# A four-mixer decoder layer with a mixture of experts: expert-weight loads held back behind the first gathered rows, and the last tile's normed rows made by VectorE

## The chip, the cores and the metric

One core of one Trainium2 chip. The metric is device time in microseconds of one execution of the whole program; three runs of the kernel before gave 1354.38 us at the median (1353.21 to 1356.09). All times below count from the start of the profiled span.

## The reference, cut to what matters

The layer has one token mixer (depth is 1, so only the stick-breaking attention runs) and then a hierarchical mixture of experts over 1024 tokens of width 1024:

```
h = rms_norm(x, norm_g[0]) * (1 + sc1) + sh1
x = x + g1 * sb_mixer(h)                       # attention, 16 heads of 64, then w_out
h = rms_norm(x, norm_g[1]) * (1 + sc2) + sh2   # "h2" below: 8 tiles of 128 tokens
grp    = argmax(h @ w_grp + b_grp)             # 1 of 4 groups
top_i  = top_k(softmax(exp_logits of grp), 2)  # 2 of the group's 8 experts
y_e    = (silu(h_e @ w_gate[e]) * (h_e @ w_up[e])) @ w_down[e]     # 32 experts, d_ff 512
x = x + g2 * sum(gate * y_e)
return rms_norm(x, final_g)
```

All is float32. sh, sc and g are six rows of 1024 made from c by one matrix product. Each expert gets the tokens that chose it, 64 on average.

## The kernel before, in words

The kernel writes every engine's instructions in the order of the Python text (`tc.manual_schedule()`), and each engine and each DMA queue works through its own in that order. A tile is taken from one pool of 49 blocks of 512 KB (`free_b`, first in first out); what first writes a block waits until all earlier users of that block are done.

Attention comes first. Then `o_stream` (lines 898 to 943) walks over the 8 tiles of 128 tokens: `o_unit(t)` multiplies by w_out and makes the residual x1 (stored to DRAM by GpSimd's queue) and u = x1 times the scale row; `h2_unit(t)` makes the normed, modulated rows h2 = u * rstd + sh2 and stores them to `h2_d` in DRAM, again on GpSimd's queue; `r_logits`, `r_pick`, `r_gate`, `r_pos`, `r_slot` and `r_table` route the tile's tokens. For the last tile (t = 7) these stand alone in lines 1045 to 1060, and nothing else is left for TensorE. Then `tables` (line 1066) gives the index lists, and `gather` (line 1078) has GpSimd's queue fetch an expert's 128 rows from `h2_d` into one of three tiles `xg`. The first three gathers stand in line 1213, behind the store of the last h2 tile.

The experts' weights are cut into 192 units of two loads of 512 KB each (list `MU`, lines 858 to 863): four "gu" units (gate and up) per expert and two "dn" units (down). The order is gu of expert 0, gu of expert 1, dn of expert 0, gu of expert 2, dn of expert 1 and so on, so units 0 to 7 are gu, 8 and 9 are dn of expert 0, 10 to 13 gu of expert 2. `m_load(n)` issues the two loads on SyncE's queue. `m_fill(reserve, upto)` loads further units while blocks are free; in `o_stream` (line 942) and in line 1047 it stops at LFIRST = 13 units, in the main loop (lines 1225, 1244) it goes on to the end, to a reserve of four.

`m_split(n)` splits a unit's two tiles into a high and a low part (ScalarE casts, line 121, VectorE subtracts, line 124), since each product is three matmuls. `xt_unit(e)` transposes the gathered rows and splits them too (lines 1107, 1109, 1110). The main loop (lines 1221 to 1250) takes unit n: 12 matmuls on TensorE (`gu_mm`, lines 1123 to 1127, or `dn_mm`, line 1164), then `m_split(n + 2)`, then `m_fill`. At n = 8, ahead of expert 0's down product, line 1241 loads the gate row `g2r` = `mod_row(3)` on the same SyncE queue. At n = 9 `y_unit(0)` (line 1176, VectorE) multiplies expert 0's result by it and scatters it to DRAM; `m_split(10)` and `m_split(11)` stand ahead of it on VectorE, `m_split(12)` behind it.

Of the kernel before, what the change touches and what calls it, by code (L numbers as in the profile page):

```python
# [16 lines left out]
AF = mybir.ActivationFunctionType  # L17
ALU = mybir.AluOpType
# [6 lines left out]
NT = T // P  # L25
# [6 lines left out]
EPS = 1e-6  # L32
NBLK = 46
RO = 6
LFIRST = 13
LOG = ()
RM = 4
SLEAD = 2
# [23 lines left out]
def decoder_layer(ctx, tc, x, c, ada_w, ada_b, norm_g, final_g, w_in, w_out, w_grp, b_grp,  # L62
                  w_exp, b_exp, w_gate, w_up, w_down, out, dbg=None):
    nc = tc.nc
# [18 lines left out]
    def take(slots, shape, dt, nm):  # L83
        cnt[0] += 1
        if not slots:
            raise RuntimeError(f"no slot for {nm}: " + str(collections.Counter(v[3] for v in held.values() if v[1] is slots)))
        pool, tag = slots.popleft()
        t = pool.tile(list(shape), dt, tag=tag, name=f"{nm}{cnt[0]}")
        held[id(t)] = (t, slots, (pool, tag), nm)
        return t  # L90

    def free(*tiles):
        for t in tiles:
            _, slots, tag, _ = held.pop(id(t))
            slots.append(tag)

    def blk(shape=(P, 1024), dt=F32, nm="b"):
        return take(free_b, shape, dt, nm)

    def pm(shape=(P, 512), nm="pm"):  # L100
        return take(free_m, shape, F32, nm)
# [536 lines left out]
    OR, XR, OT, ROW = {}, {}, {}, {}  # L638
# [42 lines left out]
    def l_transpose(t, src, q):  # L681
        if q == 0:
            ST[t] = blk((P, ND, P), nm="sT")
        pt = pm((P, 4, P))
        for j in range(4):
            nc.tensor.transpose(pt[:, j, :], src[:, (4 * q + j) * P:(4 * q + j + 1) * P], ident)  # L686
        nc.scalar.copy(ST[t][:, 4 * q:4 * q + 4, :], pt)
        free(pt)
# [57 lines left out]
    def h2_unit(t):  # L746
        u, rstd = H2[t]
        h2 = blk(nm="h2")
        if t < NT - 1:
            nc.vector.scalar_tensor_tensor(h2, u, rstd, ROW["sh2"], op0=ALU.mult, op1=ALU.add)  # L750
        else:
            nc.scalar.activation(h2, u, AF.Copy, scale=rstd)
            nc.gpsimd.tensor_tensor(h2, h2, ROW["sh2"], op=ALU.add)
        nc.gpsimd.dma_start(h2_d[t * P:(t + 1) * P, :], h2)
        if dbg == "h2":
            nc.sync.dma_start(out[0, t * P:(t + 1) * P, :], h2)
        free(h2)
# [106 lines left out]
    RAW = {}  # L864
    SPL = {}

    def m_load(n):
        if n >= len(MU):
            return
        kind, e, q = MU[n]  # L870
        rs = []
        for j in range(2):
            if kind == "gu":
                r = blk((P, 2, 512), nm="wr")
                nc.sync.dma_start(r, (w_gate, w_up)[j][0, e, q * 256:(q + 1) * 256, :].rearrange(
                    "(p k) f -> p k f", p=P))
            else:
                r = blk(nm="wr")
                nc.sync.dma_start(r, w_down[0, e, (q + j) * P:(q + j + 1) * P, :])
            rs.append(r)  # L880
        RAW[n] = rs

    nload = [0]

    def m_fill(reserve, upto=LFIRST):
        while len(free_b) - 2 >= reserve and nload[0] < min(upto, len(MU)):
            m_load(nload[0])
            nload[0] += 1

    def m_split(n):  # L890
        if n >= len(MU):
            return
        rs = RAW.pop(n)
        SPL[n] = [split(r, lo_eng="g" if (n % 6 in LOG and j == 1) else "v") for j, r in enumerate(rs)]
# [3 lines left out]
    def o_stream():  # L898
        for t in range(NT):
            for k, _ in enumerate(o_unit(t)):  # L900
# [6 lines left out]
                if t == 0:  # L907
                    if k in (2, 4):
                        l_transpose("sh2", ROW["sh2"], k // 2 - 1)
                    elif k == 6:  # L910
                        pl = l_mm("sh2")
                        nc.vector.tensor_tensor(cb, pl[:, 0:40], br, op=ALU.add)
                        free(pl)
                else:
                    if k == 2:
                        h2_unit(t - 1)
                    elif k == 4:
                        l_transpose(t - 1, H2[t - 1][0], 1)
                    elif k == 7:
                        r_logits(t - 1)  # L920
                    elif k == 8:
                        r_pick(t - 1)
                        r_gate(t - 1)
                    if t == NT - 1 and k == 14:
                        r_pos(t - 1)
                        r_slot(t - 1)
# [24 lines left out]
    for n_, _ in enumerate(first):  # L951
        k, r = divmod(n_ - AD0, AD1)
# [91 lines left out]
        return  # L1044
    run_all(ost)
    t = NT - 1
    m_fill(0)
    l_transpose(t, H2[t][0], 1)
    h2_unit(t)
    free(*ROW.values())  # L1050
    r_logits(t)
# [26 lines left out]
    def gather(xg, idx):  # L1078
        nc.gpsimd.indirect_dma_start(out=xg[:, :], out_offset=None, in_=h2_d[:, :],  # L1079
                                     in_offset=bass.IndirectOffsetOnAxis(ap=idx, axis=0),  # L1080
                                     bounds_check=T - 1, oob_is_err=False)
# [14 lines left out]
    def x_chunk(xg, c):  # L1096

        k0 = c // 2 * 256 + c % 2
        return xg[:, k0:k0 + 255:2]

    def xt_unit(e):
        xg = xgs[e % 3]
        h, l = blk((P, ND, P), F32R, nm="xTh"), blk((P, ND, P), F32R, nm="xTl")
        for q in range(2):
            pt = pm((P, 4, P))
            for j in range(4):
                nc.tensor.transpose(pt[:, j, :], x_chunk(xg, 4 * q + j), ident)  # L1107
            sl = slice(4 * q, 4 * q + 4)
            nc.scalar.copy(h[:, sl, :], pt)  # L1109
            nc.vector.tensor_tensor(l[:, sl, :], pt, h[:, sl, :], op=ALU.subtract)  # L1110
            free(pt)
        XT[e] = (h, l)
# [104 lines left out]
    for n in range(SLEAD):  # L1217
        m_split(n)
    xt_unit(0)
    gather(xgs[0], gidx[:, 3:4])  # L1220
    for n, (kind, e, q) in enumerate(MU):
        if kind == "gu":
# [38 lines left out]
    with tc.If(nx > 0):  # L1261
        with tc.For_i(0, nx, 1) as j:
# [24 lines left out]
            for q in range(4):  # L1287
                for s, src in enumerate((w_gate, w_up)):
                    r = blk((P, 2, 512), nm="owr")
# [19 lines left out]
            for f in range(NF):  # L1309
                r = blk(nm="owr")  # L1310
# [74 lines left out]
```

## Time and profile before

| | |
|---|---|
| Median of three runs | 1354.38 us |
| The profiled execution: device time, span | 1353.67 us, 1351.9 us |
| TensorE matmul busy | 1226.3 us (91%) |
| VectorE busy | 1143.2 us (85%) |
| ScalarE, GpSimd busy | 816.3 us (60%), 307.7 us (23%) |
| Bytes moved by DMA | 306.69 MB, mean 227 GB/s |
| The expert stage | about 726 to 1304 us |

The busy share is an average over stages. The seam between attention and experts, about 704 to 728 us, is the one stretch in the middle of the program in which TensorE has little to do; the page's line of 40 slices shows it as a "6" among nines, and the granted clock there falls to 0.5 of full speed.

### The profile page before, as it was taken

How to read it: one execution, taken by the hardware profiler on the slowest of the kernel's cores; microseconds unless marked ns; L12 is line 12 of the kernel's file. 1: busy time of each engine (PE TensorE's matmuls, PEld its weight loads, DVE VectorE, ACT ScalarE, POOL GpSimd, SP SyncE). 2: the span in 40 equal slices, each digit the busy share in tenths (PEclk: the TensorE clock that was granted, in tenths of full speed). 3: DMA queues.
4: the chain of work that ended last, by engine and by line, in shares of the span. 5: the costliest groups of instructions: out<-in, count | busy, mean ns of one | idle time of the engine just before them, and what ended most of it. 6: DMA issues, size and time to landing. Idle time of an engine off the chain costs nothing.

```text
span 1351.9 us, 19350 instructions
## 1 busy us (share of the span) xinstructions
PE 1226.3 (91%) x6788; PEld 986.7 (73%) x6788; DVE 1143.2 (85%) x1485; ACT 816.3 (60%) x1177; POOL 307.7 (23%) x349
## 2 busy tenths in 40 slices
PE   3999999999999997699995999999999999999950
PEld 2886767677877775478874878888888888888840
DVE  4879989876777658967776999999999999999967
ACT  4734544555655546742225777777777777777833
POOL 2711222222222214413322232111111111111002
PEclk9898999999999999899996999999999999999985
DMA  9242434300110102467359889999999999999367
GB/s 360 82 140 67 136 99 144 122 25 28 51 44 7 42 9 105 126 231 270 125 177 366 318 322 390 386 384 396 388 381 386 377 377 387 376 383 385 139 249 293
DMA packets 123396, 306.69 MB, mean 227 GB/s; under 512 B 16976, under 2 KB 49816, under 8 KB 123296
## 3 DMA queue, kind: packets, MB, share of 16 engines
q1 hardware_dynamic: 110256, 275.99, 55.7%
q0 software_dynamic: 11776, 25.20, 5.2%
q10 hardware_dynamic: 1264, 4.23, 0.8%
q8 instruction: 54, 0.88, 0.3%
q14 instruction: 46, 0.38, 0.1%
HBM read 288.58 MB, written 33.57 MB: 238 GB/s over the span
## 4 chain that ended last, share of the span: by engine, by line
issue 37%; PE 9%; POOL 8%; DMA 2%; DVE 1%; ACT 0%; POOLq 0%; SPq 0%; DVEq 0%; ACTq 0%
POOL y_d L1086 5%; POOL xg L1079 2%; PE z L112 2%; PE z L114 2%; PE z L113 2%; PE pm L696 1%; DMA xg<-h_d,tbgi 1%; PE pm L686 1%; DMA h_d<-h 1%; DMA yb<-y_d 1%; POOL frstd L1343 0%; DMA y_d<-ys,tbsi 0%; PE pm L536 0%; PE pm L563 0%; DVE S L521 0%
## 5 line engine op out<-in xcount | busy, mean ns | idle before, releaser
L124 DVE TENSOR_TENSOR lo<-wr,hi 128x1024 fp32r<-128x1024 f32 x384 | 446.7, 1217 | 11.0 <-ACT hi L121 7.6
L121 ACT CAST hi<-wr 128x1024 fp32r<-128x1024 f32 x384 | 380.6, 1051 | 17.6 <-PE pm L1164 7.0
L521 DVE TENSOR_TENSOR_SCAN S<-S 128x128 f32<-128x128 f32 (+3 forms) x192 | 190.7, 1034 | 10.6 <-POOL S L503 8.2
L1123 PE MATMUL z<-hi,xTh 128*128 128x512 f32 x512 | 161.9, 397 | 0.2 <-ACT xTh L1109 0.2
L1125 PE MATMUL z<-lo,xTh 128*128 128x512 f32 x512 | 160.0, 393 | 1.1 <-DVE lo L124 1.0
L1127 PE MATMUL z<-hi,xTl 128*128 128x512 f32 x512 | 158.8, 391 | 0.1
L1164 PE MATMUL pm<-hi,hhl 128*128 128x512 f32 x512 | 150.2, 396 | 0.0
L537 ACT COPY aT<-pm 128x512 f32<-128x512 f32 (+2 forms) x192 | 80.8, 496 | 87.4 <-PE pm L536 86.7
L501 POOL TENSOR_SCALAR_AFFINE_SELECT S<-S 128x256 f32<-128x256 f32 x64 | 52.2, 816 | 312.7 <-ACT S L497 290.3
L1125 PEld LDWEIGHTS z<-lo,xTh 128*128 128x128 f32 x512 | 96.4, 188 | 23.5 <-DVE lo L124 2.7
L1127 PEld LDWEIGHTS z<-hi,xTl 128*128 128x128 f32 x512 | 96.3, 188 | 21.4 <-DVE xTl L1110 0.4
L112 PE MATMUL pm<-hTh,hi 128*128 128x512 f32 x256 | 108.2, 423 | 3.2 <-DVE qk L405 3.2
L1086 POOL DMA_INDIRECT y_d<-ys,tbsi x32 | 67.6, 2114 | 188.1 <-DVE ys L1176 188.1
L497 ACT ACTIVATE S<-z 128x256 f32<-128x256 f32 (+3 forms) x96 | 79.0, 823 | 50.0 <-PE z L494 17.5
L1123 PEld LDWEIGHTS z<-hi,xTh 128*128 128x128 f32 x512 | 94.1, 189 | 18.6 <-ACT xTh L1109 0.6
L1164 PEld LDWEIGHTS pm<-hi,hhl 128*128 128x128 f32 x512 | 94.1, 189 | 18.1
L1079 POOL DMA_INDIRECT xg<-h_d,tbgi x32 | 35.3, 1105 | 304.9 <-PE pm L1107 297.0
L522 DVE TENSOR_TENSOR p<-p,S 128x256 f32<-128x256 f32 (+3 forms) x96 | 96.6, 1006 | 8.8 <-DVE S L521 0.2
L536 PE MATMUL pm<-ident,p 128*128 128x128 f32 x576 | 80.2, 284 | 25.6 <-DVE p L522 18.9
L114 PE MATMUL pm<-hTh,lo 128*128 128x512 f32 x256 | 101.4, 396 | 0.2 <-POOL lo L124 0.2
L113 PE MATMUL pm<-hTl,hi 128*128 128x512 f32 x256 | 101.1, 395 | 0.0
L536 PEld LDWEIGHTS pm<-ident,p 128*128 128x128 f32 x576 | 67.5, 145 | 36.8 <-issue 22.1
(217 smaller groups left out, 2259.1 us busy)
## 6 DMA issues: line engine op xcount, KB each, us to landing
wr<-in_moe_w_gate_dram SPq DMA_DIRECT2D x128, 512.0 KB
wr<-in_moe_w_up_dram SPq DMA_DIRECT2D x128, 512.0 KB
wr<-in_moe_w_down_dram SPq DMA_DIRECT2D x128, 512.0 KB
ad<-in_ada_w_dram SPq DMA_DIRECT2D x32, 512.0 KB
ada<-in_ada_w_dram SPq DMA_DIRECT2D x16, 512.0 KB
wq<-in_sb_w_in_dram SPq DMA_DIRECT2D x16, 512.0 KB
x<-in_x_dram SPq DMA_DIRECT2D x8, 512.0 KB
wv<-in_sb_w_in_dram SPq DMA_DIRECT2D x8, 512.0 KB
```

The costliest lines, as they stand in the source:

```text
L112: nc.tensor.matmul(pt, lh, rh, start=start, stop=False)
L113: nc.tensor.matmul(pt, lh, rl, start=False, stop=False)
L114: nc.tensor.matmul(pt, ll, rh, start=False, stop=stop)
L121: nc.scalar.copy(hi, raw)
L124: (nc.vector if lo_eng == "v" else nc.gpsimd).tensor_tensor(lo, raw, hi, op=ALU.subtract)
L521: nc.vector.tensor_tensor_scan(r, r, r, s[:, h, n:n + 1], op0=ALU.mult, op1=ALU.bypass)
L536: nc.tensor.transpose(pt[:, j, :], p[:, h, j * P:(j + 1) * P], ident)
L1086: s = nc.gpsimd.indirect_dma_start(out=y2_d[:, :], out_offset=bass.IndirectOffsetOnAxis(ap=idx, axis=0), in_=ys[:, :], in_offset=None, bou ...
L1123: nc.tensor.matmul(gu[:, s, :], xh_[:, k, :], sp[s][0][:, k2, :], start=k == 0, stop=False)
L1125: nc.tensor.matmul(gu[:, s, :], xh_[:, k, :], sp[s][1][:, k2, :], start=False, stop=False)
L1127: nc.tensor.matmul(gu[:, s, :], xl_[:, k, :], sp[s][0][:, k2, :], start=False, stop=k == ND - 1)
L1164: nc.tensor.matmul(py[nh], a[:, f, :], sp[j][b][:, ns], start=f == 0 and a is hth and b == 0, stop=f == NF - 1 and a is htl)
```

## The change

Four edits. LFIRST becomes 8, so that the loads ahead of the routing stop at units 0 to 7. The call `m_fill(0)` ahead of the last tile goes. Behind `xt_unit(0)` units 8 to 12 are loaded by `m_load(n, True)`, which first has VectorE write one column of zeros into each block: the load of that block is then ordered behind that write, and the write stands on VectorE behind the split of the first gathered rows. And h2 of the last tile is made as that of the other seven, by one VectorE operation, in place of ScalarE and then GpSimd.

```diff
-LFIRST = 13
+LFIRST = 8
+LHOLD = 13
     def h2_unit(t):
         u, rstd = H2[t]
         h2 = blk(nm="h2")
-        if t < NT - 1:
-            nc.vector.scalar_tensor_tensor(h2, u, rstd, ROW["sh2"], op0=ALU.mult, op1=ALU.add)
-        else:
-            nc.scalar.activation(h2, u, AF.Copy, scale=rstd)
-            nc.gpsimd.tensor_tensor(h2, h2, ROW["sh2"], op=ALU.add)
+        nc.vector.scalar_tensor_tensor(h2, u, rstd, ROW["sh2"], op0=ALU.mult, op1=ALU.add)
         nc.gpsimd.dma_start(h2_d[t * P:(t + 1) * P, :], h2)
-    def m_load(n):
+    def m_load(n, hold=False):
...
                 r = blk((P, 2, 512), nm="wr")
+                if hold:
+                    nc.vector.memset(r[:, 0, 0:1], 0.0)
                 nc.sync.dma_start(r, (w_gate, w_up)[j][0, e, q * 256:(q + 1) * 256, :].rearrange(
...
                 r = blk(nm="wr")
+                if hold:
+                    nc.vector.memset(r[:, 0:1], 0.0)
                 nc.sync.dma_start(r, w_down[0, e, (q + j) * P:(q + j + 1) * P, :])
...
     t = NT - 1
-    m_fill(0)
     l_transpose(t, H2[t][0], 1)
...
     xt_unit(0)
+    while nload[0] < LHOLD:
+        m_load(nload[0], True)
+        nload[0] += 1
     gather(xgs[0], gidx[:, 3:4])
```

## Rows read from the trace of the kernel before

**Rows 1.** Stretches: length, busy by engine with counts, granted clock, DMA share, GB/s.
```profile
718.00:727.00 9.00, 0.51 (x3) 0.54 (x4) 3.78 (x4) 0.83 (x1) 4.08 (x3) 0.50 1.03 411
...
730.00:732.00 2.00, 2.00 (x7) 1.54 (x7) 1.96 (x2) 0.99 (x3) 0.00 (x0) 0.71 0.57 221
...
765.00:775.00 10.00, 10.00 (x50) 8.14 (x49) 9.79 (x14) 6.92 (x9) 3.59 (x2) 1.00 0.99 361
...
900.00:950.00 50.00, 50.00 (x239) 41.73 (x238) 49.03 (x52) 39.18 (x46) 8.25 (x6) 1.00 1.01 387
```

**Rows 2.** Chain that ended last, across the seam: start, duration, what.
```profile
705.61 0.55 POOL rstd L742
...
707.64 2.34 POOL h L753
...
710.27 6.98 DMA h_d<-h
```

**Rows 3.** Timeline of the seam, all engines: start, duration, instruction, [idle before <-releaser].
```profile
708.97 1.04 DVE L783 TENSOR_SCALAR inl<-iogrp,gf 128x32 f32<-128x32 f32 x1
...
714.12 0.19 DVE L1070 SCALAR_TENSOR_TENSOR tbgi<-tbl,tbw 128x32 int32<-128x32 f32 x1
...
717.16 4.62 DVE L124 TENSOR_TENSOR lo<-wr,hi 128x1024 fp32r<-128x1024 f32 x4
718.14 1.21 POOL L1079 DMA_INDIRECT xg<-h_d,tbgi  x1 [7.28 <-DMA h_d<-h]
...
726.49 1.95 PE L1107 MATMUL pm<-ident,xg 128*128 128x128 f32 x8 [9.48 <-DMA xg<-h_d,tbgi]
...
728.26 1.22 PE L1123 MATMUL z<-hi,xTh 128*128 128x512 f32 x2
```

**Rows 4.** Timeline of an earlier tile's routing, VectorE.
```profile
655.72 0.24 DVE L783 TENSOR_SCALAR inl<-iogrp,gf 128x32 f32<-128x32 f32 x1
```

**Rows 5.** DMAs by tile: an x1 store at 690 us, a gather at 742 us.
```profile
L733 POOL DMA_DIRECT2D x_d<-x x1: 559/559/559, 690.3 to 690.3; - x1
DMA to landing us min/median/max: 2.9/2.9/2.9
...
L1079 POOL DMA_INDIRECT xg<-h_d,tbgi x1: 992/992/992, 742.2 to 742.2; - x1
DMA to landing us min/median/max: 4.7/4.7/4.7
```

**Rows 6.** Timeline of SyncE's DMA queue: issues of weight loads and of g2r.
```profile
693.39 8.40 SPq L879 DMA_DIRECT2D wr<-in_moe_w_down_dram  x4
...
754.13 0.42 SPq L875 DMA_DIRECT2D wr<-in_moe_w_up_dram  x1
754.64 0.38 SPq L630 DMA_DIRECT2D g2r<-mod_d  x1
```

**Rows 7.** Timelines of VectorE and TensorE around expert 0's result.
```profile
761.55 1.41 DVE L1176 SCALAR_TENSOR_TENSOR ys<-pm,tbl,g2r 128x512 f32<-128x512 f32 x2
762.87 4.62 DVE L124 TENSOR_TENSOR lo<-wr,hi 128x1024 fp32r<-128x1024 f32 x4
...
766.56 0.63 PE L1125 MATMUL z<-lo,xTh 128*128 128x512 f32 x2
...
780.27 0.50 PE L1125 MATMUL z<-lo,xTh 128*128 128x512 f32 x1 [0.63 <-DVE lo L124]
```

**Rows 8.** Timeline of the last stage: four loads queued one behind another, the fourth's use.
```profile
1309.78 0.34 SPq L1329 DMA_DIRECT2D ya<-y_d  x1
...
1311.17 0.37 SPq L1330 DMA_DIRECT2D yb<-y_d  x1
...
1318.23 1.22 DVE L1337 TENSOR_TENSOR x<-yb,ya 128x1024 f32<-128x1024 f32 x1
```

**Rows 9.** VectorE groups by shape: busy, mean ns of one, idle before.
```profile
L750 DVE SCALAR_TENSOR_TENSOR h<-u,rstd,sh2r 128x1024 f32<-128x1024 f32 x7 | 9.0, 1280 | 0.7 <-POOL rstd L742 0.7
...
L132 DVE MEMSET ones<- 128x1 f32 x1 | 0.1, 59 | 0.7 <-PEq L1374 0.7
```

## The prediction

> **What bounds the kernel now.** I read the stretches first [rows 1]. In the expert stage (900 to 950 us) TensorE is busy for 50.00 of 50 us, VectorE for 49.03, and the DMA engines' share is 1.01: TensorE sets the pace, VectorE is 2% behind, and a delay of either is not made up. In the seam (718 to 727 us) TensorE does 0.51 us of work while DMA moves 411 GB/s. The chain of waits [rows 2] and the timeline of all engines [rows 3] say why. The last tile's rstd is ready at 706.16 (705.61 + 0.55), GpSimd has h2 ready at 709.98, its store takes 6.98 us; the first gather starts at 718.14, having waited 7.28 us for that store; TensorE transposes the gathered rows from 726.49, and the first expert matmul starts at 728.26, which I call T0. Then I read SyncE's queue [rows 6], which nobody in the seam waits for: from 693.39 to 754.13 it issues 34 loads, units 8 to 24, and right behind them, at 754.64, g2r. VectorE multiplies expert 0's result by g2r at 761.55, T0 + 33.3, with no wait shown [rows 7].
>
> **The change, part by part.**
>
> *h2 by VectorE.* ScalarE's cast and GpSimd's addition go; one VectorE operation of 1.28 us [rows 9] starts when rstd is there, 706.2 to 706.3, and ends at about 707.55, where GpSimd ended at 709.98: the store starts 2.4 us earlier. VectorE loses nothing, since its next work, the routing chain, starts behind the logits at about 708. The chain also gains: its step L783 took 1.04 us and ended just when GpSimd's addition did [rows 2, 3], against 0.24 us in an earlier tile [rows 4]. The index list, ready at 714.31 before, is ready 0.8 us earlier, at 713.5.
>
> *No loads in the seam.* The store lasted 6.98 us among weight loads; an x1 store of the same 512 KB with little beside it took 2.9 us [rows 5]. At 3 to 4 us h2 lands by 711.8, ahead of the index list: that is late next. The gather starts at about 713.9 (713.5 and 0.4 of handing over), 4.2 us earlier than 718.14. It took 8.3 us (718.14 to 726.49) with DMA full; one at 742 us took 4.7 [rows 5]. I take 4.7, which has the traffic nearest to the new one; with 8.3 as the other end it lands between 718.6 and 722.2. The matmuls start 1.8 us behind it, as before (726.49 to 728.26): T0 becomes 720.4, and 7.9 us are won there.
>
> *The gate.* The ten memsets stand on VectorE behind the two splits of units 0 and 1 and the split of the gathered rows. The first takes 4.62 us from 717.16 [rows 3], now from 716.4 to 721.0; the second is two operations of 128x512, at 0.7 us each (two of that shape take 1.41 us in rows 7), so the first memset comes at about 722.4. Memsets are short (59 ns for 128x1, rows 9), some 0.6 to 1 us in all; the lo part of unit 2, queued behind them, is wanted some 7 us behind T0, so that costs nothing. If the gather takes its other end, all this is some 3 us later. SyncE's loads start there, and bytes flow about 1 us later, 723.5 (an allowance).
>
> *What that queues.* This is the step that decides. The number of units loaded ahead of g2r in the text is set by counting blocks, not by time: the fill takes blocks down to the same reserve in every step, and behind the held loads unit 12 is the last loaded, as it was before. So again units up to 24 stand ahead of g2r: 17 units of 1.049 MB, 17.83 MB, and g2r's own 0.52 MB. Three gathers pass in the same time at some 0.26 MB each (of the page's 25.20 MB on the software queue, 8.39 MB are 16 stores of 512 KB; the rest over 64 gathers and scatters). Sum 19.1 MB. At 411 GB/s [rows 1] that is 46.5 us: 770.0. That a queue serves its loads in order the last stage shows: the fourth of the loads issued from 1309.78 on, itself issued at 1311.17, is used at 1318.23 [rows 8], 8.4 us behind the first issue, where 4 x 0.524 MB at 411 GB/s with 1 us to start would give 6.1. Some of that comes from loads behind it; I add 1.3 us. g2r is then there at 771.3.
>
> VectorE comes to that multiplication at T0 + 33.3 = 753.7 and stands still until 771.4. Queued behind it are the splits of unit 12 and all later ones; units 10 and 11 are split ahead of it, so TensorE goes on through them and stops about 759. In the trace of before VectorE's sequence from 761.55 on has hardly a gap (9.79 of 10 us in 765 to 775, rows 1), and TensorE is waiting for its lo parts at 780.27 [rows 7], so there TensorE has no slack: the sequence starts 771.4 - 761.55 = 9.85 us later than before, and the rest of the program with it. The 7.9 us won at T0 are lost inside the standstill.
>
> *The clock.* Behind an idle stretch TensorE starts at half clock: granted 0.50 (1.2 GHz) in 718 to 727, and 0.71 on average in 730 to 732 [rows 1], so the step to 2.4 GHz came at about 731, 4.7 us behind 726.49. After a standstill of 15 us the same 4.7 us cost 2.35 us of TensorE's work. It restarts when unit 12's lo parts are there, 771.4 + 1.3 + 2.4 = 775.1, where it was at 766.56: 8.5 us later, and with the clock 10.9. Most of the 1.05 us over 9.85 is covered by the waits for VectorE that TensorE had anyway (0.63 us at 780.27 and shorter ones). I charge 0.35 us.
>
> The sum: 9.85 + 0.35 = 10.2 us. The profiled execution took 1353.67 us, of it 1351.9 span; it becomes 1363.9. The median of the runs shown is 0.7 us above that execution, so the forecast is 1364.6 us.
>
> A rule of the Trainium skill bears on the rate: rows show 411 GB/s in the seam and 387 in the expert stage. DMA: Bandwidth & Descriptors, Anatomy of one DMA, puts the moving of a transfer at bytes / 436e9 plus about 2 us fixed. By it 19.1 MB would be an estimated 43.8 us, g2r would come 2.7 us earlier and the time would be 1361.9; I take the row, since no stretch read here reached that rate. The same page's Rules for kernel authors advise issuing a DMA early and waiting for it late, which speaks against holding the loads; the row of g2r's issue says what else is held with them.
>
> **The bounds.** Early end: 420 GB/s, nothing for interleaving, a free clock: 723.5 + 45.5 = 769.0, 7.45 us later than before, 1361.8; a gate 1 us earlier than I think, 1360.8. Late end: 387 GB/s (49.4 us), the late gather (3 us) cut to 2 for the part of it that could fall together, 2 us for interleaving and the whole clock (1.05): 723.5 + 2 + 49.4 + 2 = 776.9, 15.4 + 1.05 = 16.4 us later, 1370.8. Not all of these fall together.
>
> **The rivals.**
>
> 1. *g2r is no hindrance.* Were it there by T0 + 33.3 = 753.8, the whole gain at T0 would stay: 7.9 us less some 0.3 for the memsets, 1346.8. That takes at most 30.3 us of transfers behind the gate, 12.4 MB at 411 GB/s, ten units and the rest, where I count 17. For it speaks that the seam's waits are read plainly from the rows, and that before g2r lands with time to spare, within 6.9 us of its issue [rows 6, 7]; against it the count of 34 loads. Chance 8%.
>
> 2. *A part of the queue passes g2r, or the gate opens earlier.* The break-even is g2r at 761.55, and what lies between gives 1354 to 1361: for 1358 it must be there at about 765, two or three units fewer. Chance 5% for slower than 1357.1, and 3% for times within 0.2%.
>
> 3. *The hold does not hold.* If the loads started in the seam as before, the contention would stay, and only the earlier h2 would count: at most the 2.4 us of the store's earlier start, 1352.0, within 0.2%. The order on VectorE speaks against it. Chance 1%.
>
> 4. *The weights themselves run out.* Unit 8 should land some 6 us behind T0 and is wanted for its split some 17 us behind it (six units of twelve matmuls at some 0.23 us), so the ten held loads have to come one at a time, at 2.9 us each in place of 1.28, to matter: g2r then comes 16 us later still, near 1381. Chance 3%.
>
> The forecast's case has 80%. Together: slower by over 0.2% (2.7 us, about what a measurement of this kernel can tell from no change) 0.88, within 0.2% 0.04, faster 0.08. The range that holds 8 in 10 is the forecast case's own, 1360.5 to 1370.
>
> **What would show it.** Right: the first gather starts near 714 and lands in under 6 us; the first expert matmul is near 720.5; no weight load is issued between 694 and 722; VectorE then has one wait of 14 to 20 us for DMA at line 1176's counterpart for expert 0, ended by g2r at 768 to 776; TensorE idles from about 759 to 775 with the clock at 0.5, and everything behind keeps its old distances. Wrong: no such wait (rival 1), a wait of VectorE or ScalarE on a weight load (rival 4), or a first gather that still starts behind 717 (rival 3). The forecast falls if fewer than about 14 units stand ahead of g2r in SyncE's queue, or if g2r lands much earlier than its place in it says.

## The result, and the profile after

The changed kernel takes 1366.32 us at the median of four runs (1363.50 to 1368.12), the kernel before 1354.35 in the same series: a ratio of 1.0085, 95% interval 1.0064 to 1.0107. It is slower by 12 us; the forecast was 1364.6. The profiled execution took 1367.35 us, its span is 1365.5 us, 13.6 more than before.

The seam in the timeline of the changed kernel (start, duration, instruction, idle before and what ended it). In these rows PE is TensorE, DVE VectorE, POOL GpSimd and SPq SyncE's DMA queue; L and a number is a line of the kernel's text. This execution comes to the seam 0.71 us earlier than that of before (rstd starts at 704.90, where [rows 2] have 705.61), so 0.71 is to be added where a time is held against the forecast's:

```profile
704.90 0.55 POOL L743 TENSOR_TENSOR rstd<-ms,mhalf 128x1 f32<-128x1 f32 x1 [0.39 <-DVE ms L741]
705.49 1.28 DVE L750 SCALAR_TENSOR_TENSOR h<-u,rstd,sh2r 128x1024 f32<-128x1024 f32 x1 [0.67 <-POOL rstd L743]
707.07 0.58 POOL L751 DMA_DIRECT2D h_d<-h  x1 [1.61 <-DVE h L750]
707.94 0.24 DVE L780 TENSOR_SCALAR inl<-iogrp,gf 128x32 f32<-128x32 f32 x1
712.29 0.19 DVE L1071 SCALAR_TENSOR_TENSOR tbgi<-tbl,tbw 128x32 int32<-128x32 f32 x1
713.34 1.10 POOL L1080 DMA_INDIRECT xg<-h_d,tbgi  x1 [5.69 <-DVE e L811]
717.89 1.95 PE L1108 MATMUL pm<-ident,xg 128*128 128x128 f32 x8 [2.71 <-DMA xg<-h_d,tbgi]
719.66 1.22 PE L1124 MATMUL z<-hi,xTh 128*128 128x512 f32 x2
...
721.14 0.08 DVE L880 MEMSET wr<- 128x1 f32 x4
721.17 0.17 DVE L874 MEMSET wr<- 128x1 f32 x6
721.26 1.89 SPq L881 DMA_DIRECT2D wr<-in_moe_w_down_dram  x4
```

The gather now waits for VectorE, where it waited for the store [rows 3]; the profile names L811, a VectorE operation a little behind the index list of L1071. The gather lands 4.55 us behind its start, where that took 8.35. From rstd's start to the first expert matmul it is 14.76 us, and was 22.65: the seam is 7.89 us shorter. Right behind the memsets SyncE begins with the held loads. Some 40 us later its queue, VectorE's timeline, and TensorE's around the standstill show this:

```profile
760.59 0.33 SPq L875 DMA_DIRECT2D wr<-in_moe_w_up_dram  x1
761.92 0.33 SPq L631 DMA_DIRECT2D g2r<-mod_d  x1
```
```profile
751.28 2.35 DVE L125 TENSOR_TENSOR lo<-wr,hi 128x1024 fp32r<-128x1024 f32 x2
772.20 1.41 DVE L1177 SCALAR_TENSOR_TENSOR ys<-pm,tbl,g2r 128x512 f32<-128x512 f32 x2 [18.57 <-DMA g2r<-mod_d]
773.53 4.62 DVE L125 TENSOR_TENSOR lo<-wr,hi 128x1024 fp32r<-128x1024 f32 x4
```
```profile
757.99 0.71 PE L1124 MATMUL z<-hi,xTh 128*128 128x512 f32 x2
774.80 0.80 PE L1126 MATMUL z<-lo,xTh 128*128 128x512 f32 x1 [16.10 <-DVE lo L125]
775.93 0.80 PE L1126 MATMUL z<-lo,xTh 128*128 128x512 f32 x1 [0.34 <-DVE lo L125]
```

The reader is to see the order: VectorE has split unit 11 and stands still for 18.57 us for one load of 512 KB, g2r; TensorE does the two units that are split, starts unit 12 with its high part, and waits 16.10 us for the low one. The rows of stretches and clock that go with it (length, busy of TensorE, its weight loads, VectorE, ScalarE, GpSimd, granted clock, DMA share, GB/s):

```profile
740.00:750.00 10.00, 10.00 (x52) 8.49 (x50) 8.82 (x9) 7.94 (x10) 0.13 (x1) 1.00 1.03 411
...
760.00:765.00 5.00, 0.00 (x0) 0.00 (x0) 0.00 (x0) 0.00 (x0) 0.00 (x0) 0.66 1.03 413
765.00:770.00 5.00, 0.00 (x0) 0.00 (x0) 0.00 (x0) 0.00 (x0) 0.00 (x0) 0.50 1.02 407
...
774.00:776.00 2.00, 0.86 (x2) 0.36 (x2) 2.00 (x3) 1.22 (x2) 1.84 (x2) 0.50 0.99 395
776.00:778.00 2.00, 2.00 (x5) 1.61 (x6) 2.00 (x2) 1.25 (x2) 0.00 (x0) 0.50 0.67 260
778.00:780.00 2.00, 2.00 (x9) 1.60 (x8) 2.00 (x4) 1.47 (x2) 0.00 (x0) 0.83 0.41 164
```

From 760 to 770 all four compute engines are idle while DMA is full at 407 to 413 GB/s, with weights that nobody wants yet. When TensorE comes back at 774.80 it has the half clock (0.50, 1.2 GHz) up to about 778.7, some 4 us.

The last expert's result in the kernel before and in the changed one:

```profile
1304.40 1.41 DVE L1176 SCALAR_TENSOR_TENSOR ys<-pm,tbl,g2r 128x512 f32<-128x512 f32 x2 [3.22 <-PE pm L1164]
```
```profile
1315.89 1.41 DVE L1177 SCALAR_TENSOR_TENSOR ys<-pm,tbl,g2r 128x512 f32<-128x512 f32 x2 [3.17 <-PE pm L1165]
```

Where the 13.6 us of span come from, read from the same rows of both traces: 0.71 us less ahead of the seam; 11.36 more from rstd's start to expert 0's result (67.30 against 55.94 us); 0.84 more from there to the last expert's result (1315.89 - 772.20 = 543.69 us; before 1304.40 - 761.55 = 542.85); 2.1 more behind it (from the last expert's result to the end of the span). That last stretch lasted 46.8 to 49.6 us in the ten traces of this study, whatever had been changed, and rstd's start lay between 702.8 and 706.7: these two are the scatter of single executions.

### The profile page after: what moved, and what is told of

The parts are those of the page before. It is cut to its first block, busy times and chain, and to the rows that moved or that the text cites. A ratio compares the mean times of both kernels' runs of the same rounds, so it can differ in the third digit from the quotient of the medians.

```text
span 1365.5 us, 19358 instructions
## 1 busy us (share of the span) xinstructions
PE 1230.2 (90%) x6788; PEld 989.6 (72%) x6788; DVE 1145.5 (84%) x1496; ACT 815.3 (60%) x1176; POOL 300.2 (22%) x348
## 4 chain that ended last, share of the span: by engine, by line
issue 38%; PE 9%; POOL 7%; DMA 1%; DVE 1%; POOLq 0%; ACT 0%; SPq 0%; ACTq 0%; DVEq 0%
POOL y_d L1087 5%; POOL xg L1080 2%; PE z L113 2%; PE z L115 2%; PE z L114 2%; PE pm L697 1%; PE pm L687 1%; DMA yb<-y_d 1%; PE pm L564 0%; POOL frstd L1347 0%; PE pm L537 0%; DMA xg<-h_d,tbgi 0%; DMA y_d<-ys,tbsi 0%; PE tblp L843 0%; PE z L495 0%
## 5 line engine op out<-in xcount | busy, mean ns | idle before, releaser
L1087 POOL DMA_INDIRECT y_d<-ys,tbsi x32 | 64.2, 2007 | 206.9 <-DVE ys L1177 206.9
```

What stands on the lines that cost most here:

```text
L1087: s = nc.gpsimd.indirect_dma_start(out=y2_d[:, :], out_offset=bass.IndirectOffsetOnAxis(ap=idx, axis=0), in_=ys[:, :], in_offset=None, bou ...
```

## The experiments

Each kernel ran beside the kernel before on one chip; ratios are to that, with their 95% intervals.

**1. The gate row first.** The changed kernel, with g2r asked for ahead of the held loads.

```diff
     xt_unit(0)
+    g2r = mod_row(3, "g2r")
     while nload[0] < LHOLD:
...
-                if e == 0:
-                    g2r = mod_row(3, "g2r")
```

> The changed kernel with one load moved: the gate row g2r is asked for just ahead of the held loads (units 8 to 12) instead of behind unit 24. Theory (the row's place in the queue is the whole loss): the 18.6 us wait of VectorE at expert 0's result is gone, TensorE runs through from its first expert matmul at about 719.7 us, and the 7.9 us won at the seam stay: 1354.4 - 7.9 = about 1346.5 us, 20 us under the changed kernel. Rival (holding 1 MB units back starves the expert stage, and the row is only where it shows first): the wait moves to a split that waits for its weight load, with most of the 18 us still there: 1358 to 1366 us.

1348.95 us (before 1353.47), ratio 0.9974 (0.9963 to 0.9985): faster than either kernel. The queue of SyncE, VectorE's and TensorE's timeline:

```profile
699.29 0.33 SPq L631 DMA_DIRECT2D g2r<-mod_d  x1
722.20 1.85 SPq L881 DMA_DIRECT2D wr<-in_moe_w_down_dram  x4
```
```profile
720.47 1.22 PE L1124 MATMUL z<-hi,xTh 128*128 128x512 f32 x2
```
```profile
752.22 2.36 DVE L125 TENSOR_TENSOR lo<-wr,hi 128x1024 fp32r<-128x1024 f32 x2
754.50 1.40 DVE L1177 SCALAR_TENSOR_TENSOR ys<-pm,tbl,g2r 128x512 f32<-128x512 f32 x2
```
```profile
1300.10 1.41 DVE L1177 SCALAR_TENSOR_TENSOR ys<-pm,tbl,g2r 128x512 f32<-128x512 f32 x2 [3.21 <-PE pm L1165]
```

The load needs no memset, so it is issued in the quiet stretch ahead of the seam. The standstill is gone and no split of this kernel waits for its weights: the rival, that holding the loads starves the stage, falls. But 1346.5 was expected. Expert 0's result is 7.05 us earlier than before, the last expert's only 4.30: the distance between the two is 545.60 us against 542.85. No wait explains it: between the two results TensorE is idle for 2.58 us in all, and for 2.66 in the kernel before. What grew is the distance from the start of one 512-column matmul to the start of the next. It is 224 to 238 ns in nearly all cases in either trace, most often 227; but of 2107 such distances (those over 300 ns left out) 823 are 231 ns or longer here, and 460 in the kernel before. Their sum is 483.77 us against 481.00, and that is the whole difference of 2.75 between the two stages. Experiments 5 and 6 go after that.

**2. The row first, nothing held.** The same move in the kernel before.

```diff
     xt_unit(0)
+    g2r = mod_row(3, "g2r")
     gather(xgs[0], gidx[:, 3:4])
...
-                if e == 0:
-                    g2r = mod_row(3, "g2r")
```

> The kernel before with the same one load moved to the same place in the text (behind the first gathered rows' split), nothing held. Theory: the row was in time before (asked for at 754.6 us, wanted at 761.6 us), so nothing changes: 1354 us, within 0.2%. Rival (the row's early place is worth something by itself, so that the first run's gain is not the hold's): 1350 us or less.

1356.15 us, ratio 1.0014 (1.0002 to 1.0026): no gain, rather 0.1% lost. So the first experiment's gain does not come from the row's early place by itself. The seam is as before (22.71 us from rstd's start to the first expert matmul), and the small loss is again along the experts: 544.07 us from the first result to the last.

**3. Three units fewer ahead of the row.** The changed kernel, with g2r asked for at n = 5.

```diff
     for n, (kind, e, q) in enumerate(MU):
+        if n == 5:
+            g2r = mod_row(3, "g2r")
...
-                if e == 0:
-                    g2r = mod_row(3, "g2r")
```

> The changed kernel with the gate row asked for behind unit 21 instead of unit 24, so three units (3.15 MB) fewer ahead of it; one weight unit is loaded a step later for the block that the row takes. Theory (loads are served in their order at about 410 GB/s): the row lands 3 x 2.56 = 7.7 us earlier, near 764.4 us, VectorE waits 11 us instead of 18.6, and the time is 1366.3 - 7.7 = about 1358.6 us. Rival (the row's own transfer is slow, 128 partitions reading one row, and its place matters little): the wait shrinks by less than 3 us, 1363 us or more.

1359.53 us, ratio 1.0052 (1.0039 to 1.0065). VectorE's wait:

```profile
765.42 1.41 DVE L1177 SCALAR_TENSOR_TENSOR ys<-pm,tbl,g2r 128x512 f32<-128x512 f32 x2 [12.25 <-DMA g2r<-mod_d]
```

The wait was expected at 11 us and the time at 1358.6. From rstd's start to this row it is 59.47 us, against 67.30 in the changed kernel: 7.83 us for three units, 2.61 per unit, where 1.049 MB at 410 GB/s take 2.56. When the row is there follows from the bytes ahead of it in the queue. The rival, a slow transfer of the row itself, falls.

**4. The VectorE operation alone.** The kernel before with the second part of the change.

```diff
-        if t < NT - 1:
-            nc.vector.scalar_tensor_tensor(h2, u, rstd, ROW["sh2"], op0=ALU.mult, op1=ALU.add)
-        else:
-            nc.scalar.activation(h2, u, AF.Copy, scale=rstd)
-            nc.gpsimd.tensor_tensor(h2, h2, ROW["sh2"], op=ALU.add)
+        nc.vector.scalar_tensor_tensor(h2, u, rstd, ROW["sh2"], op0=ALU.mult, op1=ALU.add)
```

> The kernel before with the other part of the change alone: the last tile's normed rows made by one VectorE operation, weight loads as before. Theory: the store of these rows starts 2.4 us earlier but still shares the DMA engines with the loads (5 to 7 us to landing), and the first gather still takes about 8 us: T0 comes 2 to 3 us earlier, 1351.5 to 1352.5 us. Rival (loads that fill the queue in the meantime take the lead back, since the queue is full either way and the gather lands at the same moment): 1354 us, unchanged.

1352.33 us, as expected, but ratio 0.9992 (0.9982 to 1.0001): the times alone do not tell it from nothing. The timeline does:

```profile
706.73 0.55 POOL L742 TENSOR_TENSOR rstd<-ms,mhalf 128x1 f32<-128x1 f32 x1 [0.39 <-DVE ms L740]
708.90 0.58 POOL L750 DMA_DIRECT2D h_d<-h  x1 [1.62 <-DVE h L749]
717.31 1.10 POOL L1075 DMA_INDIRECT xg<-h_d,tbgi  x1 [7.84 <-DMA h_d<-h]
725.64 1.95 PE L1103 MATMUL pm<-ident,xg 128*128 128x128 f32 x8 [8.47 <-DMA xg<-h_d,tbgi]
727.41 1.22 PE L1119 MATMUL z<-hi,xTh 128*128 128x512 f32 x2
```

20.68 us from rstd's start to the first expert matmul, against 22.65: 1.97 us won, with the gather still waiting for the store and still taking 8.3 us. From the first result to the last it is 542.84 us, and 542.85 before: this kernel's tiles lie in the same blocks.

**5. The hold and the row, with h2 made as before.** Experiment 1 with the two-engine h2 put back.

```diff
-        nc.vector.scalar_tensor_tensor(h2, u, rstd, ROW["sh2"], op0=ALU.mult, op1=ALU.add)
+        if t < NT - 1:
+            nc.vector.scalar_tensor_tensor(h2, u, rstd, ROW["sh2"], op0=ALU.mult, op1=ALU.add)
+        else:
+            nc.scalar.activation(h2, u, AF.Copy, scale=rstd)
+            nc.gpsimd.tensor_tensor(h2, h2, ROW["sh2"], op=ALU.add)
```

> The first experiment's kernel (gate row ahead of the held loads) with the last tile's normed rows made as before, by ScalarE and then GpSimd. Theory: with no load in the seam the store is no longer what the gather waits for, the index list is; so the VectorE operation is worth only the 0.8 us that the routing step under GpSimd's addition lost, and a little where the store lands last (store issued 2.4 us later, landing some 3 us behind, near 714 us): the first gather starts 0.8 to 1.5 us later and the time is 1349.0 + 1 = about 1350 us. Rival (the store is what the gather waits for in either kernel): 2.4 us later, 1351.4 us.

1348.66 us, ratio 0.9960 (0.9945 to 0.9975), not to be told from experiment 1.

```profile
706.22 0.55 POOL L743 TENSOR_TENSOR rstd<-ms,mhalf 128x1 f32<-128x1 f32 x1 [0.39 <-DVE ms L741]
714.73 0.19 DVE L1075 SCALAR_TENSOR_TENSOR tbgi<-tbl,tbw 128x32 int32<-128x32 f32 x1
715.21 1.10 POOL L1084 DMA_INDIRECT xg<-h_d,tbgi  x1 [3.76 <-DVE dm L808]
721.66 1.22 PE L1128 MATMUL z<-hi,xTh 128*128 128x512 f32 x2
...
755.45 1.40 DVE L1181 SCALAR_TENSOR_TENSOR ys<-pm,tbl,g2r 128x512 f32<-128x512 f32 x2
...
1301.07 1.41 DVE L1181 SCALAR_TENSOR_TENSOR ys<-pm,tbl,g2r 128x512 f32<-128x512 f32 x2 [3.22 <-PE pm L1169]
```

The gather waits for VectorE here too and not for the store, and the seam is 15.44 us long against 14.86 in experiment 1: 0.58 us, less than the 0.8 to 1.5 expected. Counted from rstd's start the index list is ready 0.86 us later than in experiment 1, but the gather starts only 0.30 later: it follows the end of the list by 0.29 us, where that took 0.85. What the gather waits for in those 0.85 us is not shown. Once no load runs in the seam the VectorE operation is worth half a microsecond. The distance along the experts is 545.62 us, and experiment 1 has 545.60: the same blocks, the same distance to 0.02 us, in two executions of two kernels.

**6. Other blocks.** One line ahead of the expert loop turns the list of free blocks, by one place in the kernel before and in experiment 1's kernel, and by three places in the latter. No instruction and no transfer is added or moved in the text.

```diff
     gather(xgs[0], gidx[:, 3:4])
+    free_b.rotate(-1)        # -3 in the last
     for n, (kind, e, q) in enumerate(MU):
```

> The kernel before, with the list of free blocks turned by one place at the start of the expert loop: the same instructions on every engine and queue, other blocks for the expert stage's tiles. In the first experiment TensorE's matmuls came 1% further apart for some experts without any wait (7.05 us ahead at expert 0's result, 4.3 us ahead at the last); in the kernel before they do not. Theory (where the tiles lie sets that pitch): the result of the last expert comes at a distance from expert 0's that differs from before's 742.85 us by 0.5 to 3 us, 1354 to 1357 us in time. Rival (a weight queue that never gets ahead again, as in the first experiment, slows the matmuls): the distance stays within 0.3 us and the time at 1353.5 us.

> The first experiment's kernel with the same turn of the list of free blocks by one place. Theory (blocks): the 2.75 us that it lost along the expert stage change by half a microsecond or more either way; the seam and expert 0's result stay as they were (T0 near 720.4, result near 754.5). Rival (the queue that never gets ahead): the same 2.75 us again, 1349 us.

> The same with a turn of three places. Theory (blocks): another loss along the expert stage than the 2.75 us, not the same as with one place; if one of the two is near zero the time is about 1346.5 us. Rival (the queue): 2.75 us again, 1349 us.

(The 742.85 us in the first of these is a slip for 542.85.)

| kernel | time, us | ratio to before (95%) | first to last result, us |
|---|---|---|---|
| before | 1354.09 | | 542.85 |
| before, turned by 1 | 1354.14 | 1.0003 (0.9990 to 1.0015) | 544.06 |
| experiment 1 | 1348.95 | 0.9974 (0.9963 to 0.9985) | 545.60 |
| experiment 1, turned by 1 | 1347.29 | 0.9953 (0.9936 to 0.9969) | 545.33 |
| experiment 1, turned by 3 | 1345.68 | 0.9937 (0.9918 to 0.9956) | 544.56 |

Experiment 1 ran in an earlier series, beside 1353.47 us of the kernel before; 542.85 is from the first trace of the kernel before. The rows that the column rests on, for the kernel before turned by one place, and for experiment 1's turned by three:

```profile
759.65 1.40 DVE L1176 SCALAR_TENSOR_TENSOR ys<-pm,tbl,g2r 128x512 f32<-128x512 f32 x2
1303.71 1.41 DVE L1176 SCALAR_TENSOR_TENSOR ys<-pm,tbl,g2r 128x512 f32<-128x512 f32 x2 [3.22 <-PE pm L1164]
```
```profile
753.80 1.40 DVE L1177 SCALAR_TENSOR_TENSOR ys<-pm,tbl,g2r 128x512 f32<-128x512 f32 x2
1298.36 1.41 DVE L1177 SCALAR_TENSOR_TENSOR ys<-pm,tbl,g2r 128x512 f32<-128x512 f32 x2 [3.17 <-PE pm L1165]
```

Turning alone lengthens the stage of the kernel before by 1.21 us, with the same instructions in the same order. TensorE waits no longer there (2.64 us, where it was 2.66), and the distances between its 512-column matmuls add up to 1.24 us more. So which blocks the tiles lie in sets part of the stage's length. (The seam of this execution is longer too, 23.80 us against 22.65; why is not shown.) Turning by one place moved experiment 1 by 0.27 us only, less than the half microsecond expected, and by three places 1.04. That is less than the whole 2.75.

The rival is a queue that never gets ahead. Between 850 and 1250 us SyncE's queue waits for 294 us on loads that have to land and for 14 on blocks that have to come free in experiment 1; in the kernel before it is 124 and 184. Experiment 3 speaks against the rival: its queue is ahead (59 us on loads, 239 on blocks), and still it takes 545.00 us from the first result to the last, 2.15 more than the kernel before, of which only 0.36 falls ahead of expert 1's result. Experiment 1 turned by three, with a queue that is never ahead (292 and 15), takes 544.56. So such a queue is not needed for the loss; whether it adds to it is not shown.

The median of the kernel before turned by one place is not longer than before's: single executions scatter by more than 1.2 us, and the difference is seen in the traced stage alone, in one trace of each kernel. The last kernel of the table has the lowest median of the study, though its interval overlaps that of the turn by one place.

## Why the prediction was right

**The seam.** h2's store was to start 2.4 us earlier: it starts 2.17 us behind rstd's start, where it was 4.66 (2.49 won). The routing step under GpSimd's addition was to fall from 1.04 to 0.24 us: it did. The first gather was forecast at 713.9 and starts at 714.05 on the forecast's count. Here two small misses nearly cancel, by luck: the index list is ready at 713.19, where 713.5 was forecast, and the gather follows it by 0.86 us, where 0.4 was allowed. Its landing was put at 4.7 us and took 4.55; T0 was put at 720.4 and is 720.37.

**The gate.** Forecast at 722.4, measured at 721.85 (721.14 + 0.71), half a microsecond early.

**The queue.** The step that was called deciding held: 34 loads, units 8 to 24, go out ahead of g2r, none between 693 and 721, at 404 to 416 GB/s in the stretches from 725 to 774. g2r was to let VectorE go on at 771.4; it did at 772.9 on that count, 1.5 us later, because the queue needed 2.1 us more than the 47.8 of the forecast, from a gate half a microsecond early. The rate was right; what was too small is the term of 1.3 us for loads behind g2r. From the memsets at 721.2 to g2r's use 19.44 MB passed on SyncE's queue, and 34 loads with g2r are 18.35; the other 1.09 MB, loads behind g2r, are worth 2.7 us at 411 GB/s. The rest of the 2.1 us is not worked out. Experiment 1 shows the cause, since with the row ahead of the held loads the wait is gone, and experiment 3 shows that the wait follows the number of units ahead. By the rule of the Trainium skill (DMA: Bandwidth & Descriptors, Anatomy of one DMA), bytes / 436e9 for the moving, which the page gives for DMAs issued from GpSimd, the row would have come, as an estimate that leaves out the page's 2 us fixed, 2.7 us before the forecast and 4.2 before the measurement. The rows decide against it here.

**The passing on.** VectorE's sequence was to start 9.85 us later than before; counted from rstd it starts 11.36 us later. The step that TensorE has no slack there is borne out: the results of experts 1, 2 and 3 come 10.66, 10.66 and 10.65 us later than before, as expert 0's does (10.65). The clock: half speed for some 4 us, and no further shift to be seen at expert 1's result, so the 0.35 us charged for it were too much here. In experiment 3 TensorE came back at 768.02, half speed lasted to about 773.1, 5.1 us, and from expert 0's result to expert 1's it takes 0.36 us longer than in the kernel before; there the charge would have fitted.

**What was left out.** 0.84 us along the experts, which no step of the forecast had. It is no wait: from expert 1's result on the distances between 512-column matmuls add up to 465.07 us, and to 464.30 in the kernel before. That the held loads take other blocks (experiment 6) fits this, but was not tested apart for this kernel. With it the path is 11.36 + 0.84 = 12.2 us longer, where 10.2 was forecast and the medians differ by 12.0.

**The rivals.** That g2r is no hindrance (1346.8) is what experiment 1 made of the kernel, with 1348.95; it needed an edit that the change does not have. That a part of the queue passes g2r, that the hold does not hold, and that the weights run out, are refuted by the rows above: 34 loads go out ahead of g2r, none in the seam, and VectorE's long wait ends with g2r and not with a weight load.

## What to carry to other kernels

A load that is held back held everything behind it in its queue here: before gating a prefetch, list what else is asked for on that queue, count the bytes that will stand ahead of each, and put whatever is wanted soonest ahead of the gate. Here one line moved turns 0.85% lost into 0.26% won. A stretch in which all compute engines idle while DMA is full is the sign to look for; here it meant that the queue was busy with loads that were wanted later than the one behind them.

## What the runs showed of the hardware

Turning the list of free blocks, so that the tiles lie elsewhere in on-chip memory, moved the expert stage by 1.21 us of 543 in the kernel before and by 1.04 us in experiment 1's, with every engine's instructions unchanged. What changed is not a wait but the distance between the starts of matmuls, by a few nanoseconds each. Between two kernels with the same blocks the stage repeats to 0.01 us (542.85 and 542.84) and 0.02 us (545.60 and 545.62). What in a block's place does it is open.

The issue of a load does not say when it will land: g2r was issued at 761.92 and used at 772.20, 10.3 us later, and in experiment 3 11.6 us later (753.86 and 765.42). Loads went out about every 1.3 us then, so some eight of them were under way at a time (an estimate from these figures).
